# The transposes behind a batch of 32x32 inverses, 22 products later on TensorE; their copies and scalings ahead of a key norm's second half

## Chip, cores and metric

The kernel runs on one core of a Trainium2 chip. The metric is device microseconds of one launch, by the median of several runs. One execution is profiled as well; its time is longer than the span of its trace by what lies around the span.

## The reference

One layer of a diffusion transformer over 1024 latent tokens and 256 context tokens, width 1024, in fp32. After a modulated RMS norm there is one input projection. Half of its columns feed a gated DeltaNet (4 heads of 128, chunked, forward and backward), the other half a neighbourhood attention (8 heads of 64). Output projection, a gated residual and a SwiGLU feed-forward network follow. What matters here:

```python
# gated DeltaNet, by chunk: the inverse of a unit triangular matrix
m = jnp.where(strict, jnp.einsum("bhncd,bhnmd->bhncm", kb, k) * decay, 0.0)
a_mat = jnp.eye(CHUNK, dtype=f32) + m
u = lax.linalg.triangular_solve(a_mat, v * beta[..., None], left_side=True, lower=True, unit_diagonal=True)
w = lax.linalg.triangular_solve(a_mat, kb * jnp.exp(gam)[..., None], left_side=True, lower=True, unit_diagonal=True)
# neighbourhood attention: q and k are normalised by head
q = rms_norm(q, q_norm_w) * NA_HEAD_DIM ** -0.5
k = rms_norm(k, k_norm_w)
```

## The kernel before

**Products.** An fp32 product is made of three products of rounded parts: hh x whi, hl x whi, hh x wlo. The input projection goes by jobs; a `Block` is 128 columns of weights against all tokens, with eight K steps. A block without context tokens makes two matmuls of 128x512 in each of the three products of a step, 48 in all; each of them is called a product below. A block fills `blk` banks of PSUM (4 in all).

**Order of the jobs.** k0 to k3, a wide job, nk0, nk1, nk2, the other wide job (the attention's values), nk3, nq0, nq1, nq2, q0, then q1 to q3, v0 to v3, nq3, z0 to z3. The nk and nq blocks are keys and queries of the attention, and are normalised. Around the change stand nk3, nq0, nq1, nq2, q0 and q1.

**A block's steps.** `mm` makes the products. `evac` copies the banks to `cacc` on ACT (L491; L506 for q). `silu` squares into `cr` (L532). `norm`, called after the next block's products, sums the squares on PE (a matmul with a constant for each piece of 256 or 512 columns), takes Ln (L549) and Exp (L551, L553) on ACT, then multiplies on DVE (L556), splits the result in two f16 halves (ACT L561 or L568, DVE L562 or L569), and sends four stores (L574) to nk_d or nq_d. Each Ln reads its piece from a PSUM bank that `bank()` gives: an "m" bank, of which there are two from nk0 on, or a "pr" bank, also two, for a key's last piece.

**Weights.** For each block SP loads `wraw` (L218, one buffer), ACT casts it to `whi` (L219), and POOL makes `wlo` (L221); `whi` and `wlo` have two buffers each.

**Behind the values.** After the second wide job, 16 copies from DRAM to DRAM (`windows`, L1095) are put out on SP's queue, two after each K step.

**Background work.** Two generators run piece by piece beside the blocks, one piece (`yield`) after each K step up to q0, three after that. `block_inverses` builds the 32x32 diagonal blocks, inverts all of them at once by a chain of 60 steps on DVE (L947, L949) in the tile N, then turns the result back with 32 transposes on PE (L106, four in each "m" bank), eight copies on DVE (L961, into WK), two stream transposes (L967) and two scalings by beta (L970) on DVE, and four stores to x_d (L969, L972). `preps` comes next: for each direction and chunk it fetches e, kk and xc (L997 to L999; xc comes from x_d), fills fx on ACT (L1011) and y on POOL (L1012), makes decays on ACT (L1015), multiplies kk by them on DVE (L1016), and runs four fx matmuls into "pr" with a copy on ACT (L1028), and three rounds of four y matmuls with copies on DVE (L1036). Two or three chunks are alive at a time.

**What sets the order.** A scheduler orders each engine's instructions by priority, which by default is program order, and then each engine runs its own list in that order. `high_priority(offset=n)` moves instructions up, `keep_in_program_order` pins an instruction to its place among the others of its engine, and `issue_after` holds instructions back until another has been placed.

Of the kernel before, what the change touches and what calls it, by code (L numbers as in the profile page):

```python
# [9 lines left out]
F32 = mybir.dt.float32  # L10
# [4 lines left out]
OP = mybir.AluOpType  # L15
# [12 lines left out]
NU = NCH * NH  # L28
# [63 lines left out]
def hybrid(ctx, tc, a, dbg):  # L92
    nc = tc.nc
    act, dve, pool, sp = nc.scalar, nc.vector, nc.gpsimd, nc.sync
# [14 lines left out]
    pe = Tensor()  # L109
# [33 lines left out]
    ident = M[C_ID]  # L143
# [27 lines left out]
    x_d = dram.tile([128, 2, 2, NU, 32], F32, name="x_d", tag="x_d")  # L171
# [17 lines left out]
    NB = const("NB", [128, 2, NCH, 4])  # L189
# [5 lines left out]
    bg = Background()  # L195
# [69 lines left out]
    fl = lambda x: x.rearrange("p a b -> p (a b)")  # L265
# [155 lines left out]
    with ExitStack() as bs:  # L421
# [32 lines left out]
        class Block:  # L454
# [79 lines left out]
            def norm(self):  # L534

                kind, acc, t0, i = self.kind, self.acc, self.t0, self.i
                if kind in "vz":
                    return
                if kind == "k":
                    sp.dma_start(kT_d[:, i], acc)  # L540
                    return
                r = self.r
                if kind == "q":
                    sp.dma_start(qT_d[:, i], acc[:, t0:])
                    return
                for s0, n in self.segs:
                    p = bank("pr" if kind == "nk" and s0 >= 768 else "m")
                    pe.matmul(p[:, :n], M[C_BD2], r[:, s0:s0 + n], start=True, stop=True)
                    act.activation(r[:, s0:s0 + n], p[:, :n], AF.Ln, bias=b_eps, scale=1.0 / ND)  # L549
                if kind == "nq":  # L550
                    act.activation(r[:, t0:], r[:, t0:], AF.Exp, scale=-0.5, bias=b_naq)  # L551
                else:
                    act.activation(r[:, t0:], r[:, t0:], AF.Exp, scale=-0.5)  # L553
                isk = kind == "nk"
                u = acc
                dve.scalar_tensor_tensor(u[:, t0:], u[:, t0:], qkw[:, isk:isk + 1], r[:, t0:],  # L556
                                         op0=OP.mult, op1=OP.mult)
                hl16 = cp.tile([128, 2, T], F16, name="hl16", tag="kx", bufs=3)
                h16, l16 = hl16[:, 0], hl16[:, 1]
                if isk:  # L560
                    act.copy(h16, u)  # L561
                    dve.tensor_tensor(l16, u, h16, OP.subtract)  # L562
                else:
                    for hf in range(2):
                        s = slice(t0 + hf * 512, t0 + hf * 512 + 512)
                        uv = u[:, s].rearrange("p (r b c) -> p b r c", r=8, b=4)
                        hv, lv = (x[:, s].rearrange("p (b r c) -> p b r c", b=4, r=8) for x in (h16, l16))
                        act.copy(hv, uv)  # L568
                        dve.tensor_tensor(lv, uv, hv, OP.subtract)  # L569
                for i, x in enumerate((h16, l16)):  # L570
                    for hb in range(2):
                        hd = 2 * self.i + hb
                        dst = nk_d[i, hd] if isk else nq_d[hd, i]
                        sp.dma_start(dst, x[hb * 64:hb * 64 + 64, t0:])  # L574
# [99 lines left out]
        first = [Block("k", 0), Block("k", 1)]  # L674
        with ExitStack() as xs:
# [12 lines left out]
            for k in range(KT):  # L688
                x = xp.tile([128, T], F32, name=f"xt{k}", tag=f"xt{k}")
# [95 lines left out]
            split = "split"  # L785
# [101 lines left out]
        def block_inverses():  # L887
            with ExitStack() as gs:
# [3 lines left out]
                N = gp.tile([128, 4, 32, 32], F32, name="N", tag="N")  # L892
                P = 2 * NU
                fl = lambda x: x.rearrange("p u i -> p (u i)")
                with ExitStack() as g3s:
# [18 lines left out]
                    for i, (d, u0, n) in enumerate(cuts):  # L914
                        rcs, nxt = nxt, rhs(*cuts[i + 1]) if i + 1 < len(cuts) else None
                        p = bank()
# [33 lines left out]
                    yield  # L950
                flat = N.rearrange("p b r c -> p b (r c)")
                dve.memset(flat[:P, :, 0:1024:33], 1.0)
                for _ in range(1):
                    yield
                U = WK.rearrange("p d u i -> p (d u) i")
                for i0 in range(0, 32, 4):
                    p = bank()
                    for i in range(4):
                        pe.transpose(p[:, i * P:(i + 1) * P], N[:P, :, :, i0 + i].rearrange("p b r -> p (b r)"),
                                     ident[:P, :P])  # L960
                    dve.tensor_copy(U[:, :, i0:i0 + 4], p[:, :4 * P].rearrange("p (i u) -> p u i", i=4))  # L961
                    if i0 % 8 == 4:
                        yield
                for d in range(2):
                    ud = U[:, d * NU:(d + 1) * NU]
                    ut = g4.tile([128, NU, 32], F32, name="ut", tag="ut")
                    dve.transpose(fl(ut), fl(ud))  # L967
                    x, s = (ut, ud) if d else (ud, ut)
                    sp.dma_start(x_d[:, d, 0], x)  # L969
                    dve.tensor_tensor(s, s, NB[:, d].rearrange("p c (h o) -> p (c h) o", o=1).to_broadcast(  # L970
                        [128, NU, 32]), OP.mult)
                    sp.dma_start(x_d[:, d, 1], s)  # L972
                    yield

        done = set()

        def preps():

            first_half.close()
            with ExitStack() as gs:  # L980
# [11 lines left out]
                def fetch(d, c):  # L992

                    kk, xc = work("kk", 5), pp.tile([128, 2, 4, 32], F32, name="xc", tag="xc", bufs=3)
                    e = work("e", 4)
                    u = (d * NCH + c) * 4
                    sp.dma_start(fl(e), g_d[u:u + 4].rearrange("h t -> (h t)").partition_broadcast(128))  # L997
                    sp.dma_start(kk, kk_d[:, c])
                    sp.dma_start(xc, x_d[:, d, :, c * 4:c * 4 + 4])  # L999
                    at = None  # L1000
                    if c >= 2:
                        at = work("at", 4)
                        sp.dma_start(at, qk_d[:, c - 2])
                    return d, c, kk, xc, e, at
# [49 lines left out]
                todo = [(d, ORDER[d][i]) for i in range(NCH) for d in range(2)]  # L1054
                live, landing = [], []
                n = 0
                while live or todo or landing:
                    while len(landing) < 2 and todo and (todo[0][1] < 2 or all(x in done for x in queries)):
                        landing.append([fetch(*todo.pop(0)), False])
                    if landing and len(live) < 3:  # L1060
                        triangle(landing[0])
                        live.append(prep(n, *landing.pop(0)[0]))
                        n += 1
                        if landing:
                            triangle(landing[0])
                    if not live:
                        yield
                    nxt = []
                    for g in live:
                        tick[0] += 1  # L1070
                        flush(tick[0])
                        if next(g, 0):
                            nxt.append(g)
                        yield
                    live = nxt
# [9 lines left out]
        values = inv + 3  # L1085
        queries = range(turn - 1, later)
        jobs += [Block("v", i) for i in range(4)] + [Block("nq", 3)]
        gates = len(jobs)
        jobs += [Block("z", i) for i in range(4)]

# [15 lines left out]
        first[0].evac()  # L1106
        first[0].silu()
        first[1].evac()
        first[0].norm()
        first[1].silu()  # L1110
        for n in range(2, len(jobs) + 2):
            j = jobs[n] if n < len(jobs) else None
# [27 lines left out]
            if isinstance(j, Wide):  # L1140
                for t, _ in enumerate(j.tiles()):
                    next(fin, 0)
                    for _ in range(3):
                        next(taps, 0)
                    if t == 4 and nrm:
                        nrm.norm()
                        for _ in fin:
                            pass
                        fin = nrm.finish()
                        done.add(n - 1)  # L1150
                        nrm = None
                    bg2.step(2)
                    if n < turn:
                        bg.step(2)
                    if n >= turn:
                        bg.step(5)
            elif j:
                for k in range(KT):
                    j.mm([k])
                    next(taps, 0)  # L1160
                    next(taps, 0)
                    if k >= 3:
                        next(fin, 0)
                    bg.step(1 if n < turn else 3)
                    bg2.step(1)
                    copies.step(2)
                j.evac()
            for _ in fin:
                pass
# [1 line left out]
            if isinstance(j, Wide) and n == values:  # L1171
                copies.add(windows())
            if nrm:
                nrm.norm()
            if isinstance(j, Block) and j.later is None:
                j.silu()

# [395 lines left out]
    with ExitStack() as us:  # L1573
# [13 lines left out]
        def split(x, src, k):  # L1587
            act.copy(x[0][:, k], src[:, k])
            dve.tensor_tensor(x[1][:, k], src[:, k], x[0][:, k].bitcast(F32), OP.subtract)  # L1589
# [274 lines left out]
```

## Time and profile before

| what | us |
|---|---|
| runs before | 1516.0, 1511.06, 1514.58 |
| their median | 1514.58 |
| the profiled execution | 1507.78 |
| its span | 1506.0 |
| mean granted TensorE clock of the profiled execution | 0.994 of full speed |

A row of the timeline has the start and duration in us, the engine, the line and operation, output<-inputs with the tile's size and the number of instructions that it groups, and in brackets how long the engine had been idle and which instruction ended that. The span of a group covers its instructions from first to last, and matmuls overlap, so the distance of two starts says more than a duration. PE is TensorE's matrix product, DVE the vector engine, ACT the scalar engine, POOL GpSimd; SP (SPq for its queue) issues the DMAs. Lines of the profile before are those of the kernel before; in the changed kernel the same instructions stand 5 to 14 lines further down (L556 is L561, L561 is L566, L568 is L573, L961 is L968, L967 and L970 are L976 and L979, L1011 is L1021, L1016 is L1026, L1028 is L1038).

### The profile page before, as it was taken

The numbers are of one execution on the slowest core, as the hardware profiler recorded it, in microseconds if no ns is written. First come the engines' busy times: TensorE is split into PE (matmuls) and PEld (weight loads), VectorE is DVE, ScalarE is ACT, GpSimd is POOL, SyncE is SP. The second block draws the span as 40 slices with busy tenths as digits, with TensorE's granted clock in tenths as the row PEclk, the third lists the DMA queues.
The fourth block names the chain that finished last, engine by engine and source line by source line (L and its number), as shares of the span: only waits on it lengthen the run. The fifth ranks groups of instructions, "written<-read, shape, count | busy, mean of one in ns | idle before, by whom it ended". The sixth has DMA issues, their size and how long they took to land.

```text
span 1506.0 us, 23093 instructions
## 1 busy us (share of the span) xinstructions
PE 1449.8 (96%) x8365; PEld 1201.0 (80%) x8365; DVE 1004.4 (67%) x1892; ACT 696.2 (46%) x1321; POOL 193.4 (13%) x223
## 2 busy tenths in 40 slices
PE   5999998899999999999989999999999999999998
PEld 2789787678877778887877878888888888888887
DVE  4886579455598427679966499666655557698642
ACT  6443461584266526566742374333333334354440
POOL 0154500343124221211100000000000000000000
PEclk9999999999999999999999999999999999999999
DMA  9377133555377799986349106333333334898742
GB/s 368 117 234 239 57 92 121 191 168 190 118 243 238 220 284 265 262 228 193 110 134 332 72 30 203 113 105 105 102 102 105 106 105 161 287 349 286 240 145 84
DMA packets 198851, 267.35 MB, mean 178 GB/s; under 512 B 15232, under 2 KB 106960, under 8 KB 197712
## 3 DMA queue, kind: packets, MB, share of 16 engines
q1 hardware_dynamic: 198016, 265.49, 54.7%
q8 instruction: 66, 1.08, 0.3%
q14 instruction: 49, 0.40, 0.1%
q10 hardware_dynamic: 720, 0.37, 0.1%
HBM read 201.01 MB, written 68.98 MB: 179 GB/s over the span
## 4 chain that ended last, share of the span: by engine, by line
PE 51%; DVE 6%; ACT 3%; DMA 2%; issue 1%; SPq 0%; ACTq 0%; DVEq 0%
PE ps L102 45%; PE sc L102 5%; PE sc L106 2%; DMA wad<-wa 1%; ACT pt L377 1%; ACT ex L365 1%; DVE ex L363 1%; DVE acc L255 1%; DVE x L1618 1%; DVE x L1594 0%; DVE ex L367 0%; DVE ulo L1449 0%; DVE lT L1589 0%; DVE ws L1444 0%; ACT x L1598 0%
## 5 line engine op out<-in xcount | busy, mean ns | idle before, releaser
L102 PE MATMUL ps<-hT,uhi 128*128 128x512 f32 x496 | 146.8, 390 | 0.8 <-DVE e L1739 0.7
L102 PE MATMUL ps<-lT,uhi 128*128 128x512 f32 x496 | 146.4, 389 | 0.0
L102 PE MATMUL ps<-hT,ulo 128*128 128x512 f32 x496 | 146.3, 389 | 0.0
L102 PE MATMUL blk<-hh,whi 128*128 128x512 f32 (+1 forms) x456 | 138.0, 393 | 2.4 <-ACT hh L748 1.7
L102 PE MATMUL blk<-hh,wlo 128*128 128x512 f32 (+1 forms) x456 | 129.7, 377 | 0.0
L102 PE MATMUL ps<-hB,uhi 128*128 128x512 f32 x436 | 129.1, 390 | 0.0
L102 PE MATMUL blk<-hl,whi 128*128 128x512 f32 (+1 forms) x456 | 129.0, 376 | 0.0
L102 PE MATMUL ps<-lB,uhi 128*128 128x512 f32 x436 | 128.8, 389 | 0.0
L102 PE MATMUL ps<-hB,ulo 128*128 128x512 f32 x436 | 128.8, 389 | 0.0
L1448 ACT CAST uhi<-ws 128x512 fp32r<-128x512 f32 x91 | 54.7, 622 | 145.5 <-PE ps L102 78.2
L1448 ACT CAST uhi<-wq 128x512 fp32r<-128x512 f32 x101 | 60.4, 621 | 132.8 <-PE ps L102 69.4
L1449 DVE TENSOR_TENSOR ulo<-wq,uhi 128x512 fp32r<-128x512 f32 x101 | 67.1, 687 | 65.6 <-ACT uhi L1448 36.4
L102 PEld LDWEIGHTS ps<-hT,uhi 128*128 128x128 f32 x496 | 93.0, 188 | 20.7 <-ACT uhi L1448 1.1
L102 PEld LDWEIGHTS ps<-lT,uhi 128*128 128x128 f32 x496 | 93.0, 188 | 19.7 <-DVE lT L1602 0.5
L102 PEld LDWEIGHTS ps<-hT,ulo 128*128 128x128 f32 x496 | 93.1, 188 | 19.4
L102 PEld LDWEIGHTS ps<-hB,uhi 128*128 128x128 f32 x436 | 81.8, 188 | 17.5 <-issue 0.5
L102 PEld LDWEIGHTS ps<-lB,uhi 128*128 128x128 f32 x436 | 81.8, 188 | 17.3 <-DVE lB L1602 0.4
L102 PEld LDWEIGHTS ps<-hB,ulo 128*128 128x128 f32 x436 | 81.8, 188 | 17.0
L102 PEld LDWEIGHTS blk<-hh,wlo 128*128 128x128 f32 x456 | 80.1, 189 | 17.6 <-issue 1.7
L102 PEld LDWEIGHTS blk<-hl,whi 128*128 128x128 f32 x456 | 80.7, 189 | 15.5
L102 PEld LDWEIGHTS blk<-hh,whi 128*128 128x128 f32 x456 | 76.5, 189 | 19.8 <-ACT hh L748 3.7
L1449 DVE TENSOR_TENSOR ulo<-ws,uhi 128x512 fp32r<-128x512 f32 x91 | 60.6, 685 | 36.2 <-ACT uhi L1448 28.0
(341 smaller groups left out, 3026.0 us busy)
## 6 DMA issues: line engine op xcount, KB each, us to landing
wq<-w_fo SPq DMA_DIRECT2D x99, 256.0 KB
wq<-w_gu SPq DMA_DIRECT2D x88, 256.0 KB
wad<-wa SPq DMA_DIRECT2D x64, 256.0 KB
t_d<-g SPq DMA_DIRECT2D x22, 512.0 KB
fr<-t_d SPq DMA_DIRECT2D x44, 256.0 KB
bt<-rpb SPq DMA_DIRECT2D x48, 192.0 KB
f_d<-g SPq DMA_DIRECT2D x33, 256.0 KB
fr<-f_d SPq DMA_DIRECT2D x33, 256.0 KB
```

Source lines behind the costliest of these rows:

```text
L102: i = nc.tensor.matmul(*args, **kw)
L106: i = nc.tensor.transpose(*args, **kw)
L255: dve.scalar_tensor_tensor(acc2, x, sc, acc2, op0=OP.mult, op1=OP.add)
L363: dve.tensor_tensor_reduce(ex, sc, bt, 1.0, -3.0e38, OP.add, OP.max, m[:, 0:1])
L365: act.activation(ex, ex, AF.Exp, bias=m[:, 1:2], accum_out=m[:, 2:3])
L377: act.copy(pt, sc)
L1448: act.copy(hi, self.raw[key])
L1449: dve.tensor_tensor(lo, self.raw[key], hi.bitcast(F32), OP.subtract)
L1618: dve.tensor_tensor(B[at][:, k], B[x][:, k], B.get(y, B["B11"])[:, k], OP.subtract)
```

## The change

The transposes leave eight pieces after the inverses' last step instead of one, and are pinned to program order; their copies, the stream transposes and the scalings get a higher priority. The stream transposes write into N's memory instead of a new tile. `norm` is cut in two: the part up to the Exp, and `split`, which multiplies, casts and stores. While the inverses aren't done, nk3's `split` is kept back until the first chunk's fetch has been put into the program, and then follows the last scaling; for the other blocks up to q0 `split` follows the last scaling too. The first two chunks' fetches come ahead of the rest of `preps` by three pieces, and from q1 on a block's last K step runs four pieces of background work.

```diff
-                isk = kind == "nk"
+                return self.split
+
+            def split(self):
+
+                acc, t0, i, r = self.acc, self.t0, self.i, self.r
+                isk = self.kind == "nk"
                 u = acc
                 dve.scalar_tensor_tensor(u[:, t0:], u[:, t0:], qkw[:, isk:isk + 1], r[:, t0:],
                                          op0=OP.mult, op1=OP.mult)
...
-                for _ in range(1):
+                for _ in range(8):
                     yield
                 U = WK.rearrange("p d u i -> p (d u) i")
                 for i0 in range(0, 32, 4):
                     p = bank()
                     for i in range(4):
-                        pe.transpose(p[:, i * P:(i + 1) * P], N[:P, :, :, i0 + i].rearrange("p b r -> p (b r)"),
-                                     ident[:P, :P])
-                    dve.tensor_copy(U[:, :, i0:i0 + 4], p[:, :4 * P].rearrange("p (i u) -> p u i", i=4))
+                        tc.keep_in_program_order(nc.tensor.transpose(
+                            p[:, i * P:(i + 1) * P], N[:P, :, :, i0 + i].rearrange("p b r -> p (b r)"),
+                            ident[:P, :P]))
+                    with tc.high_priority(offset=400):
+                        dve.tensor_copy(U[:, :, i0:i0 + 4], p[:, :4 * P].rearrange("p (i u) -> p u i", i=4))
                     if i0 % 8 == 4:
                         yield
-                for d in range(2):
-                    ud = U[:, d * NU:(d + 1) * NU]
-                    ut = g4.tile([128, NU, 32], F32, name="ut", tag="ut")
-                    dve.transpose(fl(ut), fl(ud))
...
-                    yield
+                with tc.high_priority(offset=400):
+                    for d in range(2):
+                        ud = U[:, d * NU:(d + 1) * NU]
+                        ut = N.rearrange("p b r c -> p (b r c)")[:, d * 1280:(d + 1) * 1280].rearrange(
+                            "p (u i) -> p u i", i=32)
+                        dve.transpose(fl(ut), fl(ud))
+                        x, s = (ut, ud) if d else (ud, ut)
+                        sp.dma_start(x_d[:, d, 0], x)
+                        end = dve.tensor_tensor(s, s, NB[:, d].rearrange("p c (h o) -> p (c h) o", o=1).to_broadcast(
+                            [128, NU, 32]), OP.mult)
+                        sp.dma_start(x_d[:, d, 1], s)
+                inverse[:] = [end]
+                yield
...
-                    sp.dma_start(xc, x_d[:, d, :, c * 4:c * 4 + 4])
+                    started.append(sp.dma_start(xc, x_d[:, d, :, c * 4:c * 4 + 4]))
...
+                landing += [[fetch(*todo.pop(0)), False] for _ in range(2)]
+                for _ in range(3):
+                    yield
                 while live or todo or landing:
...
-                    bg.step(1 if n < turn else 3)
+                    bg.step(1 if n < turn else 4 if k == 7 else 3)
                     bg2.step(1)
                     copies.step(2)
+                if waiting:
+                    while not started:
+                        bg.step(1)
+                    with tc.issue_after(inverse[0].ins):
+                        waiting.pop()()
                 j.evac()
...
             if nrm:
-                nrm.norm()
+                rest = nrm.norm()
+                if nrm is tail and not inverse:
+                    waiting.append(rest)
+                else:
+                    with tc.issue_after(inverse[0].ins) if inverse and n < turn else ExitStack():
+                        rest()
```

Here `tail` is nk3. The other two calls, `first[0].norm()` and the one in the wide job, become `norm()()`.

The first place is on PE, at the end of nq0's products and the start of nq1's. Before (hh_136 begins a block, so the last rows are nk3's norm and the first products of nq1):

```order
L102 MATMUL blk<-hh_419,whi 128x512 x2
L106 MATMUL m<-cst,N 128x80 x2
L102 MATMUL blk<-hl_420,whi 128x512 x2
L102 MATMUL blk<-hh_419,wlo 128x512
L106 MATMUL m<-cst,N 128x80 x6
L102 MATMUL blk<-hh_419,wlo 128x512
...
L102 MATMUL blk<-hh_423,wlo 128x512 x2
L102 MATMUL m<-cr,cst 128x256
L102 MATMUL m<-cr,cst 128x512
L102 MATMUL pr<-cr,cst 128x512
L102 MATMUL blk<-hh_136,whi 128x512 x2
```

In the changed kernel, from the end of nq0:

```order
L102 MATMUL blk<-hh_423,wlo 128x512 x2
L102 MATMUL m<-cr,cst 128x256
L102 MATMUL m<-cr,cst 128x512
L102 MATMUL pr<-cr,cst 128x512
L102 MATMUL blk<-hh_136,whi 128x512 x2
L102 MATMUL blk<-hl_137,whi 128x512 x2
L102 MATMUL blk<-hh_136,wlo 128x512 x2
L964 MATMUL m<-cst,N 128x80 x8
L102 MATMUL blk<-hh_138,whi 128x512 x2
L102 MATMUL blk<-hl_139,whi 128x512 x2
L102 MATMUL blk<-hh_138,wlo 128x512 x2
L964 MATMUL m<-cst,N 128x80 x8
```

The transposes have moved from ahead of nk3's norm to behind it, with 16 products of nq0 and six of nq1 in front; two more groups of eight follow after six products each.

The second place is on ACT, from the cast of nq2's weights to the first chunk's decays. In the changed kernel:

```order
L219 CAST whi<-wraw 128x1024
L491 ACTIVATE cacc<-blk 128x512 x2
L549 ACT_TABLE_LOAD
L549 ACTIVATE cr<-m,bias 128x256
L549 ACTIVATE cr<-m,bias 128x512
...
L219 CAST whi<-wraw 128x1024
L549 ACT_TABLE_LOAD
L549 ACTIVATE cr<-m,bias 128x512 x2
L551 ACT_TABLE_LOAD
L551 ACTIVATE cr<-cr,bias 128x1024
L566 CAST hl_2568<-cacc 128x1280
L573 CAST hl_2586<-cacc 128x512 x2
```

and what follows it there, with the evacuation and the square of nq1 between the chunk's pieces:

```order
L491 ACTIVATE cacc<-blk 128x512 x2
L1021 COPY fx_2535<-xc 32x4x32
L532 ACTIVATE cr<-cacc 128x1024
L1021 COPY fx_2535<-xc 32x4x32 x3
L1025 ACTIVATE e<-e,GN 128x128 x4
```

Up to L549 of nk3 the order is that of before. Behind it, before has L561, L219, L491, L549, L551 and then the chunk's copies; now nk3's cast follows nq0's Exp, and nq1's evacuation stands ahead of the chunk.

More of the change, by code (lines that the diff above doesn't have):

```diff
@@ L537, in norm @@
                 if kind in "vz":
-                    return
+                    return int
                 if kind == "k":
                     sp.dma_start(kT_d[:, i], acc)
-                    return
+                    return int
                 r = self.r
@@ L544, in norm @@
                     sp.dma_start(qT_d[:, i], acc[:, t0:])
-                    return
+                    return int
                 for s0, n in self.segs:
@@ L958, in block_inverses @@
                     for i in range(4):
-                        pe.transpose(p[:, i * P:(i + 1) * P], N[:P, :, :, i0 + i].rearrange("p b r -> p (b r)"),
-                                     ident[:P, :P])
-                    dve.tensor_copy(U[:, :, i0:i0 + 4], p[:, :4 * P].rearrange("p (i u) -> p u i", i=4))
+                        tc.keep_in_program_order(nc.tensor.transpose(
[3 more added lines that the diff above has]
+                        dve.tensor_copy(U[:, :, i0:i0 + 4], p[:, :4 * P].rearrange("p (i u) -> p u i", i=4))
                     if i0 % 8 == 4:
                         yield
-                for d in range(2):
-                    ud = U[:, d * NU:(d + 1) * NU]
-                    ut = g4.tile([128, NU, 32], F32, name="ut", tag="ut")
-                    dve.transpose(fl(ut), fl(ud))
[L968 to L972, printed above, removed]
-                    yield
-        done = set()
+                with tc.high_priority(offset=400):
[11 more added lines that the diff above has]
+                yield
+        done, inverse, waiting, started = set(), [], [], []
         def preps():
@@ L1087, in hybrid @@
         jobs += [Block("v", i) for i in range(4)] + [Block("nq", 3)]
+        tail = jobs[values + 1]
         gates = len(jobs)
@@ L1108, in hybrid @@
         first[1].evac()
-        first[0].norm()
+        first[0].norm()()
         first[1].silu()
@@ L1145, in hybrid @@
                     if t == 4 and nrm:
-                        nrm.norm()
+                        nrm.norm()()
                         for _ in fin:
@@ L1173, in hybrid @@
             if nrm:
-                nrm.norm()
+                rest = nrm.norm()
[4 more added lines that the diff above has]
+                        rest()
             if isinstance(j, Block) and j.later is None:
```

## The prediction

> **What bounds the kernel now.** I read the page's first part, then the list of what TensorE (PE) waits for, then the timelines of PE, ACT, DVE and SP around the two waits that the change aims at, and last the granted clock there.
>
> ```profile
> span 1506.0 us, 23093 instructions
> PE 1449.8 (96%) x8365; PEld 1201.0 (80%) x8365; DVE 1004.4 (67%) x1892; ACT 696.2 (46%) x1321; POOL 193.4 (13%) x223
> ```
>
> PE is busy for 96% of the span, so time comes off only where PE idles or runs at half clock. In the list of waits (in all, times, longest) two belong to the inverses and the chunk preparation:
>
> ```profile
> PE pr L102 <- DVE kk L1016: 6.9, 1, 6.9
> PE m L106 <- DVE N L952: 5.4, 1, 5.4
> ```
>
> The first of them in time stands inside the block nq0 (start, duration, what runs, and in brackets the idle time before):
>
> ```profile
> 256.38 0.61 PE L102 MATMUL blk<-hh,whi 128*128 128x512 f32 x2
> 262.41 0.53 PE L106 MATMUL m<-cst,N 80*128 80x80 f32 x2 [5.42 <-DVE N L952]
> 262.67 1.20 PE L102 MATMUL blk<-hl,whi 128*128 128x512 f32 x2
> 263.67 0.63 PE L102 MATMUL blk<-hh,wlo 128*128 128x512 f32 x1
> ...
> 267.06 0.48 PE L102 MATMUL blk<-hl,whi 128*128 128x512 f32 x1
> ...
> 267.74 0.49 PE L102 MATMUL blk<-hl,whi 128*128 128x512 f32 x1
> ...
> 271.27 1.45 PE L102 MATMUL m<-cr,cst 128*128 128x256 f32 x4
> ...
> 273.02 1.04 PE L102 MATMUL blk<-hh,whi 128*128 128x512 f32 x2
> 273.90 0.63 PE L102 MATMUL blk<-hl,whi 128*128 128x512 f32 x2
> 274.37 0.62 PE L102 MATMUL blk<-hh,wlo 128*128 128x512 f32 x2
> ```
>
> Five sizes come out of these starts. A warm pair of products takes about 0.455 (0.47 from 273.90 to 274.37), a product 0.2275. A cold pair takes 1.00 (262.67 to 263.67). Four transposes and a product take 0.68 (267.06 to 267.74), so eight transposes about 0.9. The norm of nk3 takes 1.75 (271.27 to 273.02). From 262.41 to 271.27 there are 32 transposes and 16 products: 8.86, of which the products are worth 16 x 0.2275 = 3.64, so transposes and cold clock cost 5.22.
>
> The second wait stands at the first chunk's matmuls, in nq2:
>
> ```profile
> 284.37 1.88 PE L102 MATMUL m<-cr,cst 128*128 128x512 f32 x4
> 299.09 2.02 PE L102 MATMUL pr<-fx,kk 128*128 128x96 f32 x8 [6.90 <-DVE kk L1016]
> ...
> 309.41 1.03 PE L102 MATMUL pr<-fx,kk 128*128 128x96 f32 x8
> 310.37 0.85 PE L102 MATMUL pr<-y,kk 128*32 128x96 f32 x8
> ...
> 315.15 1.03 PE L102 MATMUL blk<-hh,whi 128*128 128x512 f32 x2
> ```
>
> So the stretch that the change can touch runs from 256.38 to 315.15, where q0 starts. The granted clock in it, by single microseconds (the number behind the busy times is the clock):
>
> ```profile
> 259.00:260.00 1.00, 0.00 (x0) 0.00 (x0) 0.94 (x2) 0.00 (x0) 0.00 (x0) 0.82 0.26 100
> 266.00:267.00 1.00, 1.00 (x10) 0.98 (x9) 0.40 (x1) 0.00 (x0) 0.00 (x0) 0.76 0.80 264
> 297.00:298.00 1.00, 0.00 (x0) 0.00 (x0) 0.00 (x0) 1.00 (x5) 0.49 (x1) 0.60 1.02 338
> ```
>
> A share of 0.82 means full speed until 259.64, which is 2.6 us after PE stopped at 262.41 - 5.42 = 256.99; in the second wait the drop came at 297.2, 5.0 us after the stop at 292.19. After the restart at 262.41 full speed came back at about 266.5, 4.1 us later.
>
> **First part: the transposes.** Behind hh,whi at 256.38, which ends its slot at 256.83, PE now goes straight on: 16 products (3.64) to 260.47, nk3's norm (1.75) to 262.2, six products of nq1 (1.37) to 263.6. The wait of 5.42 is gone by then, since N's chain ended on DVE about 263. But what is late next is the place that the transposes write to. They take an "m" bank; there are two, and by the new order nk3's norm has just filled both. They come free when ACT's L549 has read them. ACT:
>
> ```profile
> 273.49 1.05 ACT L219 CAST whi<-wraw 128x1024 fp32r<-128x1024 f32 x1 [20.93 <-DMA wraw<-w_nqk]
> 274.45 1.08 ACT L491 ACTIVATE cacc<-blk 128x512 f32<-128x512 f32 x2
> 275.54 1.28 ACT L549 ACT_TABLE_LOAD   x1
> 276.83 1.05 ACT L549 ACTIVATE cr<-m,bias 128x256 f32<-128x256 f32 x2
> ```
>
> L549 stands in ACT's order, before and after, behind the cast of nq2's weights, and that one waited 20.93 us for their load. What holds the load is on SP's queue:
>
> ```profile
> 249.66 11.61 SPq L1095 DMA_DIRECT2D vw_d<-nv_d  x5
> 261.36 2.26 SPq L218 DMA_DIRECT2D wraw<-w_nqk  x1
> ```
>
> The window copies vw_d go out ahead of it in both versions; the change moves neither. In before nobody noticed: the transposes ran ahead of nk3's norm, when the banks were empty. Now they stand behind it, so PE waits from 263.6 to about 277.2 (the first of the two L549 is the short one, about 0.4): **13.6 us in place of 5.42**. Queued behind them on PE is the rest of nq1, 42 products, and all after it.
>
> From 277.2: eight transposes, the second bank coming free at 277.9, to about 278.4; six products at half clock (3.0) to 281.4, where the clock is back (277.2 + 4.1); then 24 transposes (2.0 to 2.7) and 36 products (8.19) to 291.6 to 292.3. I take 292.0. Before, that point (nq1's end) was 284.37. So the first part costs **+7.6**. Its bounds: the load of nq2 landing 0.6 earlier, as the x_d stores no longer run beside its end, +7.0; transposes paced by the eight copies on DVE, +8.3. The copies (L968 now, ahead on DVE by priority) lie beside these 36 products.
>
> **Second part: the scalings, nk3's second half, the first chunks.** Before, from 284.37 to 315.15 there are 30.8 us. The work in it is about 20.3: nq0's and nq1's norms (1.75 x 1024/1280 = 1.4 each), 48 products of nq2 (10.92), and some 6.6 of chunk matmuls (for sizes see 309.41: four fx matmuls 0.96; 310.37 and below: a round of y up to 0.8). So 10.5 is overhead: 6.90 of waiting, 2 of half clock behind it, 1.6 in small pieces. What is it after? PE reaches the first fx matmuls after 1.4 of norm and 42 products (9.56) instead of 26, at 303.0. They need the copies fx and DVE's L1026, and those stand at the end of this ACT chain (durations from before):
>
> ```profile
> 283.62 1.26 ACT L561 CAST hl<-cacc 128x1280 f16<-128x1280 f32 x1 [1.62 <-DVE cacc L556]
> 288.90 1.27 ACT L549 ACTIVATE cr<-m,bias 128x512 f32<-128x512 f32 x2
> 290.06 1.06 ACT L532 ACTIVATE cr<-cacc 128x1024 f32<-128x1024 f32 x1
> 292.43 1.15 ACT L551 ACTIVATE cr<-cr,bias 128x1024 f32<-128x1024 f32 x1
> 295.35 1.25 ACT L1011 COPY fx<-xc 32x128 f32<-32x128 f32 x4 [1.77 <-DMA xc<-x_d]
> 296.63 1.57 ACT L1015 ACTIVATE e<-e,GN 128x128 f32<-128x128 f32 x5
> 301.84 1.14 ACT L568 CAST hl<-cacc 128x512 f16<-128x512 f32 x2
> ```
>
> and of DVE, whose two scalings and stream transposes (L976, L979, 1.5 each) end about 293 to 295, ahead of nk3's L561:
>
> ```profile
> 272.18 1.49 DVE L970 TENSOR_TENSOR ut<-ut,NB 128x1280 f32<-128x1280 f32 x1
> 286.32 3.70 DVE L970 TENSOR_TENSOR WK<-WK,NB 128x1280 f32<-128x1280 f32 x1
> 298.34 0.69 DVE L1016 TENSOR_TENSOR kk<-kk,e 128x512 f32<-128x512 f32 x1 [3.45 <-DMA nk_d<-hl]
> ```
>
> The cast of q0's weights waits for nq1's last product with whi, about 291.7. From there: cast 1.05, table 1.28, L549 1.27, table 1.28, L551 1.15 (297.7); nk3's cast 1.26 (299.0); nq0's casts 1.14; L491 waits for nk3's residual on DVE, which follows nq0's scaling (299.0 + 1.5), then 1.08 (301.6); L1021 and L532 2.31; four e of the row's 1.57 for five, 1.26 (305.2); L1026 0.69: **305.9**. The wait is 2.9. One L970 took 3.70 where the other took 1.49; if that repeats, it is hidden by the chain above, which DVE meets only at 297.7. Were that cover gone it would cost 2.2.
>
> Two more waits appear, as ACT's order now has the evacuation and the norm of the next block ahead of the next chunks' pieces. For the third chunk's fx: from nq2's last product ACT does L491 1.08, a copy 0.5, L532 1.06, two tables 2.56, L549 1.27, L551 1.15, four e and four fx 2.5, casts 1.14, then DVE 0.69: 11.95, against PE's 10.3 (fx 0.96, norm 1.4, 31 products 7.05, two rounds of y about 0.9). That is 1.7, 2.2 with what is left over from the first. For the fourth chunk the same kind of chain, with a weight cast and three e more, is 12.4 against 10.2: 2.2. In all 2.9 + 2.2 + 2.2 and small pieces 0.9: 8.2 in place of 10.5, **-2.3**.
>
> Moved as well: nk3's four and nq0's four stores to nk_d and nq_d now follow the first two chunks' fetches on SP's queue, and ahead of the third's.
>
> ```profile
> 290.94 0.85 SPq L999 DMA_DIRECT2D xc<-x_d  x1
> 294.97 1.11 SPq L574 DMA_DIRECT2D nk_d<-hl  x2
> ```
>
> Eight issues at 0.55 are 4.4 us, from 300 on; a fetch was used 4.4 us after its issue (290.94 to 295.35). The third chunk's data land about 309.5, and are used about 313: hidden. The attention that reads nk_d and nq_d comes much later. The first chunk's own fetch goes out behind the scalings, about 296, and lands by 300.5, ahead of L1021 at 301.6. The memory of ut now lies in N, which nobody reads by then. Behind q1 the orders are the same but for a few chunk pieces.
>
> **Clock.** A wait of 2.9 stands close to the 2.6 after which the clock fell once and under the 5.0 of the other time; 2.2 stands under both. I take nothing for it; if the first of them halves the clock it adds 2 (before's second wait), if all do, up to 4. [...]
>
> **Sum.** +7.6 - 2.3 = +5.3, with bounds of -2.9 (the second part's overhead all gone: 7.6 - 10.5) and about +12 (clock, DVE's 2.2, the upper bound of the first part). The profiled run took 1507.78 with the span of 1506.0 in it, so it would become 1513.1. It lies 6.8 under the median of the runs, 1514.58; with the same difference the median becomes **1519.9, say 1520**.
>
> **Rivals.**
> 1. The transposes wait as told, but the second part becomes smooth: chunks find their fx ready. For it: PE arrives 3.9 us later than before at the first fx (303.0 against 299.09) and the wait was 6.90 from 292.19. Against it: ACT's chain is 14.2 long from nq1's end. 7.6 - 10.5 = -2.9: 1511.7, no measurable change.
> 2. The change does what it says: both waits go, the banks are free in time. This takes L549 to have read by 263.6, 13.6 us earlier than the rows; it decides for "faster" only if nq2's weights land by about 260, with the vw_d copies still in front. -5.42 - 2 (cold) - 6.9 = -14: 1500.
> 3. As the forecast, with the small waits halving the clock and DVE's 2.2 in the open: +9 to +12, 1524 to 1527.
>
> **How the numbers follow.** Differences under about 0.3%, 4.5 us, can't be told from no change. Forecast 0.64, of it 0.45 over +4.5 and 0.19 within; rival 1 0.15, within; rival 2 0.09, faster; rival 3 0.12, slower. That makes faster 0.09, same 0.34, slower 0.57. The range goes from just below rival 1 (1510) to the upper end of rival 3 (1527), which leaves out rival 2 and some of the tails.
>
> **What would show it.** Right: a wait of 13 to 14 us of PE at the first L964 transposes, put down to ACT's L549, with half clock behind it; no wait on N; a wait of about 3 us on DVE L1026, and two of 2 us later. Wrong: L549 well before 277, transposes without a wait; or a wait of over 5 us still at the first fx. If the first wait is there and the total is no slower, the second part was mis-sized.

## The result and the profile after

| | runs | median, us | lowest to highest |
|---|---|---|---|
| before | 7 | 1511.06 | 1508.67 to 1516.0 |
| changed | 7 | 1519.26 | 1518.09 to 1525.14 |

The ratio is 1.0057, with a 95% interval of 1.0036 to 1.0078: the change makes the kernel 8.2 us slower. Forecast were +5.3 us and 1520. The profiled execution of the changed kernel took 1521.18 us, with a span of 1519.4.

What TensorE waits for in the changed kernel between 240 and 362 us (in all, times, longest):

```profile
PE m L964 <- ACT cr L549: 13.3, 1, 13.3
PE pr L102 <- DVE kk L1026: 3.5, 2, 2.5
PE pr L102 <- ACT kk L1038: 3.3, 1, 3.3
```

The waits of 5.4 and 6.9 are gone; in their place stand four. Their places in PE's timeline:

```profile
264.69 0.62 PE L102 MATMUL blk<-hh,wlo 128*128 128x512 f32 x2
278.58 1.37 PE L964 MATMUL m<-cst,N 80*128 80x80 f32 x8 [13.27 <-ACT cr L549]
279.69 1.20 PE L102 MATMUL blk<-hh,whi 128*128 128x512 f32 x2
280.68 1.05 PE L102 MATMUL blk<-hl,whi 128*128 128x512 f32 x2
...
294.14 1.88 PE L102 MATMUL m<-cr,cst 128*128 128x512 f32 x4
...
308.06 1.53 PE L102 MATMUL pr<-fx,kk 128*128 128x96 f32 x8 [2.48 <-DVE kk L1026]
...
324.75 1.10 PE L102 MATMUL pr<-fx,kk 128*128 128x96 f32 x8 [1.04 <-DVE kk L1026]
...
345.62 0.44 PE L102 MATMUL pr<-y,kk 128*32 128x32 f32 x8 [3.25 <-ACT kk L1038]
...
360.38 1.84 PE L102 MATMUL m<-ones,cr 128*128 128x1 f32 x16
```

And on ACT the cast that everything stands behind, with the load that it waits for:

```profile
250.11 1.05 ACT L219 CAST whi<-wraw 128x1024 fp32r<-128x1024 f32 x1 [13.14 <-PE blk L102]
...
274.71 1.04 ACT L219 CAST whi<-wraw 128x1024 fp32r<-128x1024 f32 x1 [20.99 <-DMA wraw<-w_nqk]
275.66 1.08 ACT L491 ACTIVATE cacc<-blk 128x512 f32<-128x512 f32 x2
276.76 1.28 ACT L549 ACT_TABLE_LOAD   x1
278.05 1.05 ACT L549 ACTIVATE cr<-m,bias 128x256 f32<-128x256 f32 x2
```

The first transposes start some 0.5 us after L549 does, and L549 starts 3.3 us after the cast. To compare traces I measure from the cast of nq1's weights (here 250.11), which stands ahead of the change, to the start of nq0's norm (294.14, where nq1 ends), and from there to the first matmul with ones in v0's part (360.38), behind which both run alike for a while. In the kernel before the two outer marks are:

```profile
248.94 1.05 ACT L219 CAST whi<-wraw 128x1024 fp32r<-128x1024 f32 x1 [13.14 <-PE blk L102]
```

```profile
349.55 1.84 PE L102 MATMUL m<-ones,cr 128*128 128x1 f32 x16
```

With 284.37 between them, before has 35.4 and 65.2 us, 100.6 in all; the changed kernel 44.0 and 66.2, 110.3 in all. So the first part costs 8.6 us and the second 1.1, together 9.7. Beyond the two outer marks the profiled runs differ by another 3.7 us: 1.2 ahead, where both kernels run the same order, and 2.6 behind. For 83.6 us behind the second mark TensorE runs the same order in the same time; then some of the chunks' matmuls come in other places, so that a part of the 2.6 may still be the change's. The medians differ by 8.2.

### The profile page after: what moved, and what is told of

Its sections match the earlier page's. It is cut to its first block, busy times and chain, and to the rows that moved or that the text cites. A ratio compares the mean times of both kernels' runs of the same rounds, so it can differ in the third digit from the quotient of the medians.

```text
span 1519.4 us, 23101 instructions
## 1 busy us (share of the span) xinstructions
PE 1453.8 (96%) x8365; PEld 1204.4 (79%) x8365; DVE 1008.0 (66%) x1892; ACT 699.5 (46%) x1323; POOL 197.4 (13%) x223
## 4 chain that ended last, share of the span: by engine, by line
PE 51%; DVE 5%; ACT 3%; DMA 2%; issue 1%; SPq 0%; ACTq 0%; DVEq 0%
PE ps L102 44%; PE sc L102 5%; PE sc L106 2%; DMA wad<-wa 1%; ACT pt L377 1%; ACT ex L365 1%; DVE acc L255 1%; DVE ex L363 1%; DVE x L1642 1%; DVE x L1618 0%; DVE ulo L1473 0%; DVE lT L1613 0%; DMA zT_d<-zt 0%; DMA wraw<-w_out 0%; ACT x L1622 0%
```

## The experiments

Two theories. **Banks**: the time goes at the transposes, which wait for the two m banks that nk3's norm holds, since L549 is queued on ACT behind a cast whose weights come late. **Second half**: the time goes where the key norm's second half and the chunks were rearranged. All results in one table; the marks are those just defined, from each kernel's profiled run, and each ratio is against the kernel before on the same chip.

| kernel | cast to nq1's end | from there to the ones | both | median, us | ratio to before (95%) |
|---|---|---|---|---|---|
| before | 35.4 | 65.2 | 100.6 | | |
| changed | 44.0 | 66.2 | 110.3 | 1519.26 | 1.0057 (1.0036 to 1.0078) |
| e1: Ln ahead of the cast | 28.8 | 71.3 | 100.1 | 1510.67 | 1.0004 (0.9989 to 1.0020) |
| e2: load ahead of the copies | 33.7 | 66.6 | 100.3 | 1510.63 | 1.0000 (0.9987 to 1.0012) |
| e3: transposes at their old place | 35.6 | 68.1 | 103.7 | 1514.71 | 1.0027 (1.0016 to 1.0038) |
| e4: before, transposes moved | 43.8 | 61.4 | 105.2 | 1513.88 | 1.0028 (1.0017 to 1.0039) |
| g1: changed, both remedies | 28.8 | 66.8 | 95.6 | 1504.71 | 0.9955 (0.9939 to 0.9971) |
| g2: e4, both remedies | 31.9 | 62.0 | 93.9 | 1502.87 | 0.9950 (0.9933 to 0.9967) |
| g3: before, both remedies | 35.5 | 68.6 | 104.1 | 1513.03 | 1.0017 (1.0000 to 1.0034) |
| g4: changed, second half at once | 44.1 | 63.1 | 107.2 | 1519.33 | 1.0061 (1.0037 to 1.0085) |
| h1: g4, both remedies | 30.6 | 65.4 | 96.0 | 1505.20 | 0.9959 (0.9942 to 0.9976) |
| h2: g2, copies by priority | 31.8 | 64.6 | 96.4 | 1504.17 | 0.9977 (0.9964 to 0.9989) |
| h3: short hold, both remedies | 28.8 | 66.6 | 95.4 | 1503.09 | 0.9957 (0.9943 to 0.9972) |
| k1: e3 without early fetches | 35.4 | 68.3 | 103.7 | 1510.49 | 1.0007 (0.9992 to 1.0021) |

The medians of before in the four series were 1510.46 (e), 1511.51 (g), 1510.29 (h) and 1510.36 (k).

**e1: nk3's Ln ahead of the cast.**

```diff
-            act.copy(h, r)
+            with tc.issue_after(hold[0].ins) if hold else ExitStack():
+                act.copy(h, r)
...
+                hold[:] = [jobs[n - 2].ln] if n == values + 3 else []
                 jobs[n + 1].prefetch()
+                hold[:] = []
```

`ln` is the norm's last L549. Expected:

> The changed kernel, with ACT's cast of nq2's weights held behind the three Ln of nk3's norm; nothing else. Theory (banks): the change costs time because the transposes wait for the two m banks that nk3's norm holds, and these are read late only because L549 stands behind that cast. Then TensorE's wait at the first transposes shrinks from 13.3 us to 0 to 1.5 us, with full clock behind it, and nq1 ends about 15 us earlier than in the changed kernel. q0's weights are loaded no earlier than before, so the chunk preparation starts late and the wait at the first fx matmuls grows from 2.5 us to about 7. In sum 9 to 10 us less than the changed kernel: about 1510. Rival (second half): the loss comes from the key norm's second half and the chunks behind it, and a wait taken away at the transposes only moves there: the wait goes but the time stays within 3 us of the changed kernel, 1517 to 1522.

PE's timeline of e1 (line numbers three higher):

```profile
265.96 0.68 PE L967 MATMUL m<-cst,N 80*128 80x80 f32 x4 [0.30 <-ACT cr L552]
...
278.83 1.88 PE L102 MATMUL m<-cr,cst 128*128 128x512 f32 x4
...
296.82 2.02 PE L102 MATMUL pr<-fx,kk 128*128 128x96 f32 x8 [6.55 <-DVE kk L1029]
```

and its ACT:

```profile
263.90 0.47 ACT L552 ACTIVATE cr<-m,bias 128x256 f32<-128x256 f32 x1
...
274.60 1.05 ACT L222 CAST whi<-wraw 128x1024 fp32r<-128x1024 f32 x1 [8.12 <-DMA wraw<-w_nqk]
...
282.62 1.05 ACT L222 CAST whi<-wraw 128x1024 fp32r<-128x1024 f32 x1 [4.38 <-DMA wraw<-w_conv]
```

The cast still comes at 274.6, but TensorE doesn't wait for it: the 13.3 shrink to 0.3, and nq1 ends 15.2 us earlier. A third of that is lost again, as expected: q0's weights go into the buffer that nq2's have just left, so their cast now waits 4.38 for its own load, and with it the first fx, 6.55. The rival, that the wait only moves, falls: the time is 8.6 us below the changed kernel's.

**e2: the load ahead of the window copies.**

```diff
                 for ch in range(4):
-                    sp.dma_start(vw_d[:, cb, ch], vlat[4 * ch:4 * ch + 4, BLKS[cb]:BLKS[cb] + 32])
+                    while cb * 4 + ch >= 11 and not ahead:
+                        yield
+                    with tc.issue_after(ahead[0].ins) if cb * 4 + ch >= 11 else ExitStack():
+                        sp.dma_start(vw_d[:, cb, ch], vlat[4 * ch:4 * ch + 4, BLKS[cb]:BLKS[cb] + 32])
                     yield
...
+                if n == values + 3:
+                    ahead[:] = loaded
```

`ahead` holds the load of nq2's weights, once it has been put out. Expected:

> The changed kernel, with the last five of the 16 window copies issued behind the load of nq2's weights instead of ahead of it; the orders on TensorE and ACT stay. Theory (banks): the load lands 8 to 11 us earlier, the cast and L549 follow it, and the wait at the first transposes shrinks by as much, from 13.3 to 2 to 5.5 us, with some half clock left. Total 8 to 11 us below the changed kernel, about 1510. Rival 1: the load is slow by itself and not because of the copies ahead of it; then it lands as late as before and the wait stays at 13. Rival 2 (second half): the wait shrinks and the total stays within 3 us of the changed kernel.

SP, ACT and PE of e2 in that order:

```profile
256.19 0.61 SPq L220 DMA_DIRECT2D wraw<-w_nqk  x1
256.85 10.08 SPq L1114 DMA_DIRECT2D vw_d<-nv_d  x5
```

```profile
264.46 1.05 ACT L221 CAST whi<-wraw 128x1024 fp32r<-128x1024 f32 x1 [10.62 <-DMA wraw<-w_nqk]
```

```profile
268.33 1.38 PE L966 MATMUL m<-cst,N 80*128 80x80 f32 x8 [2.88 <-ACT cr L551]
```

The cast moves from 274.71 to 264.46, 10.3 us earlier, and the wait shrinks by 10.4, from 13.27 to 2.88, with ACT's and PE's orders untouched. So the load's landing sets this wait, and the copies ahead of it set the landing.

**e3: only the transposes back at their old place.** The edit is `range(8)` to `range(1)` in the changed kernel.

> The changed kernel with the transposes one piece behind the inverses' last step again, so ahead of nk3's norm; priorities, the split norm and the early fetches stay. Theory (banks): no wait on L549; instead the wait of about 5.4 us on N as before the change, and nq1 ends where it did before. The chunk's copies and decays now stand ahead of nq1's evacuation on ACT, and the wait at the first fx should be about 2 us in place of 6.9. Total 3 to 6 us below the kernel before: about 1506. Rival (second half): the split and the moved fetches are what costs; then this kernel stays slower than the kernel before, 1515 or more.

This expectation missed by 9 us. The wait on N is back with 5.43, as told, but the first fx still wait 6.3:

```profile
289.98 1.88 PE L102 MATMUL m<-cr,cst 128*128 128x512 f32 x4
...
298.67 2.02 PE L102 MATMUL pr<-fx,kk 128*128 128x96 f32 x8 [6.34 <-DVE kk L1026]
```

The first chunk is ready 8.7 us behind nq1's end, against 14.7 in the kernel before (299.09 less 284.37); but TensorE now comes to it after two products of nq2 instead of 26. An earlier chunk that was also ordered earlier gains nothing, and a wait of 2.4 at the fourth chunk came on top. The rival, 1515 or more, stands closer to the 1514.71 than my figure. But only 3.0 us of it lie between the marks in the profiled run; that run also lost time well ahead of them, at a mean granted clock of 0.82 against 1.00, in code that the kernels share. The 15 us from 150 on, of e3 and of the kernel before (granted clock third from the right):

```profile
150.00:165.00 15.00, 13.19 (x61) 10.98 (x60) 10.31 (x44) 1.29 (x7) 8.14 (x13) 0.82 0.16 45
```

```profile
150.00:165.00 15.00, 14.17 (x78) 11.79 (x77) 8.06 (x40) 2.92 (x9) 8.25 (x15) 1.00 0.17 48
```

How many of e3's other runs have that, the profile of one doesn't say.

**e4: only the transposes moved.** The kernel before with `range(8)` and the pinned transposes.

> The kernel before with only the transposes moved: eight pieces instead of one, pinned to program order. Theory (banks): TensorE waits 13 us for nk3's L549 at the first transposes, just as in the changed kernel, and nq1 ends 8 to 9 us later than before. The first fx now stand behind all of nq2 and nq1's norm, so that the wait there (6.9 us before) may vanish: between 1511 and 1519, say 1515. Rival (second half): with the second half where it was, moving the transposes costs nothing: no wait over 3 us at the transposes, and a time at or below the kernel before.

```profile
277.81 1.38 PE L959 MATMUL m<-cst,N 80*128 80x80 f32 x8 [12.97 <-ACT cr L549]
...
293.44 1.88 PE L102 MATMUL m<-cr,cst 128*128 128x512 f32 x4
...
309.73 1.13 PE L102 MATMUL pr<-fx,kk 128*128 128x96 f32 x8 [1.76 <-DVE kk L1017]
```

The wait is there in full, 12.97, and so is the first part's cost (43.8 against 35.4). The fx wait falls to 1.76, since they stand behind 48 products, and the second part gives 3.8 us back. So by the medians the moved transposes alone (1.0028) cost about as much as the rest of the change alone (e3, 1.0027), and the whole change as much as both (1.0057).

**g1 to g3: both remedies, with the whole change, with the delay alone, and without any of it.**

> The changed kernel with both remedies of the first runs: ACT's cast of nq2's weights behind nk3's Ln, and the last five window copies behind the load of these weights. Theory (banks): no wait at the transposes as with the first remedy alone, and q0's weights now come in time, so that the wait at the first fx goes back from 6.5 to about 3 us. From the cast of nq1's weights to the first matmul with ones (100.6 us in the kernel before, 110.3 in the changed one) 95 us: about 1505, 5 us below the kernel before. Rival: the wait at the first fx stays at 6 or more because ACT's chain from nq1's end is the limit whatever the loads do; then 100 us and no gain over the first remedy, 1510.

> The kernel before with the transposes moved by eight pieces and pinned, and both remedies; the key norm's second half, priorities and fetches as before the change. Two theories on the second part. If the change's own second part (split norm, priorities, early fetches) costs about 5 us, as the stretch behind nq1's end says (61.4 us with the delay alone, 66.2 in the changed kernel), this kernel saves the first part's cost and that too: a stretch of 90 to 92 us, 1500 to 1502. If the short second part of the delay alone is only time won back because everything there was already late, it grows to 66 or more here and the kernel is no better than the one with both remedies on the changed kernel, 1505.

> The kernel before with both remedies and nothing of the change. If the remedies work by freeing the banks for moved transposes, they gain little here: the wait of 5.4 us on N stays, and only the wait at the first fx shrinks as ACT's chain runs earlier, from 6.9 to 3 to 5 us; 1506 to 1509. If they gain as much here as with moved transposes, the place of the transposes doesn't matter: 1500 to 1503.

g1 came out as expected: q0's cast now waits for nq1's products and not for its load, and the first fx wait 3.02 us. g2 lies close to the first of its two answers: the short second part stays (62.0), but the stretch of 93.9 and the median of 1502.87 are above the 90 to 92 and 1500 to 1502 told. Both rows are g1's:

```profile
278.22 1.05 ACT L224 CAST whi<-wraw 128x1024 fp32r<-128x1024 f32 x1 [9.07 <-PE blk L102]
```

```profile
292.45 1.13 PE L102 MATMUL pr<-fx,kk 128*128 128x96 f32 x8 [3.02 <-DVE kk L1031]
```

With the place of the transposes as in the change and the banks free, the kernel is 7 to 9 us faster than before; of the two, g2, without the rest of the change, has the lower ratio, but the intervals overlap widely. g3 was expected at 1506 to 1509 and isn't faster than before at all. The fx wait shrinks to 4.51 as told, but a later one appears, and the wait on N stays:

```profile
297.45 2.02 PE L102 MATMUL pr<-fx,kk 128*128 128x96 f32 x8 [4.51 <-DVE kk L1021]
...
337.24 1.49 PE L102 MATMUL pr<-y,kk 128*32 128x96 f32 x8 [3.04 <-DVE y L1041]
```

So the remedies gain nothing by themselves; they pay because the transposes moved.

**g4, h1: the second half at once.** In the changed kernel, without and with the remedies:

```diff
-                if nrm is tail and not inverse:
-                    waiting.append(rest)
-                else:
-                    with tc.issue_after(inverse[0].ins) if inverse and n < turn else ExitStack():
-                        rest()
+                rest()
```

> The changed kernel with nk3's second half (and nq0's) put out at once again, without the hold and without the wait for the scaling; transposes, priorities and early fetches stay changed. Wait of 13 us at the transposes in any case. If the held-back second half is what makes the second part slow, it shortens from 66.2 to 61 to 63 us, and the time goes from 1519 to about 1514 to 1515. If the early fetches and priorities do it, the time stays at 1518 to 1520.

> The changed kernel with both remedies, and the second halves of nk3's and nq0's norms put out at once, without hold. Two effects against each other, by the traces so far: held back, nk3's L561 does not stand between the transposes' copies on DVE (nq1 ends 28.8 us behind the cast of its weights, 31.9 where it stands there); but the second part is longer by 3 to 5 us. If both are real this kernel lies between the two earlier ones: nq1's end at 31 to 32, second part 62 to 63.5, 1503 to 1505. If the hold costs nothing in the second part, that stays at 66 to 67 and the time is 1507 or 1508.

By the marks the hold costs 3.1 us in the second part without the remedies (66.2 against 63.1). But g4's median, of six runs, is the changed kernel's; the question stays open there. With the remedies the two effects cancel: held back, nk3's L561 stays out of the copies' way on DVE (28.8 against 30.6), and costs 1.4 behind (66.8 against 65.4); g1 and h1 have the same time. h1's second part was told as 62 to 63.5, so here the hold costs less than half of what its trace without the remedies said. The hold is not what makes the change slow.

**h2, h3: looking for the good of both.** h2 gives g2's copies the change's priority. h3 holds nk3's second half only until the last copy, puts nq0's out at once, and has no early fetches; of its edit against g1, the first:

```diff
+                if waiting:
+                    with tc.issue_after(copied[0].ins):
+                        waiting.pop()()
```

> The kernel before with the transposes moved, both remedies, and of the change's other parts only the priority of the transposes' copies. DVE's order still has nk3's scaling behind the first two copies, so TensorE should still wait 1 to 1.5 us for a copy: nq1's end at 31 to 32, second part 62 as without the priority, 1502 to 1503. If the priority alone cures that wait: nq1's end at 29, 1500.

> Moved transposes and both remedies, nk3's second half held back only until the last of the eight copies (not until the scalings and the first fetch), nq0's second half at once, no early fetches. If the hold helps by keeping DVE free for the copies and harms by putting nk3's cast and nq1's evacuation ahead of the first chunk on ACT, this has the good of both: nq1's end at 28.8, second part 62 to 63, a stretch of 91 to 92 against 100.6 before, 1500 to 1502. If the harm comes with any hold: second part 66, 1505.

Priority alone doesn't bring nk3's L561 out from between the copies (31.8), as expected; its second part is 2.6 longer than g2's in the profile, where 62 was told. h3 has the short first part, and the second was missed (66.6 against 62 to 63): the first fx wait only 0.65, but at the fourth chunk there is

```profile
327.40 0.64 PE L102 MATMUL pr<-y,kk 128*32 128x32 f32 x8 [5.57 <-ACT kk L1042]
```

ACT's order has the next chunk's decays and another block's casts ahead of that chunk's copy, and for these decays ACT stood 3.06 us until POOL had masked e:

```profile
324.47 0.40 ACT L1029 ACTIVATE e<-e,GN 128x128 f32<-128x128 f32 x1 [3.06 <-POOL e L1058]
```

Neither beats g2.

**k1: e3 without the early fetches.**

```diff
-                landing += [[fetch(*todo.pop(0)), False] for _ in range(2)]
-                for _ in range(3):
-                    yield
...
-                    bg.step(1 if n < turn else 4 if k == 7 else 3)
+                    bg.step(1 if n < turn else 3)
```

> The changed kernel with the transposes one piece behind the inverses' last step, and without the early fetches, their three pieces and the fourth piece of a last K step: of the change only priorities, the memory of ut and the hold are left. Asked is what in the rest of the change costs some 4 us when the transposes stay. If it is the early fetches, which let the chunks' pieces spread behind the next block's evacuation on ACT, the wait of 2.4 at the fourth chunk goes and the second part returns from 68 to 65 or 66 us: 1510 to 1512. If it is the priority, which draws the scalings and with them the first fx ahead on TensorE, the second part stays at 67 to 69: 1514. The wait of 6.3 at the first fx should stay in both cases, since these stand behind two products of nq2 in either.

The time came out as the first answer had it, and the stretch as the second: 1510.49, but 68.3 us in the second part, with 7.86 at the first fx. So between the marks k1 and e3 are alike (103.7 both), and the 4 us by which their medians differ lie elsewhere or in runs that weren't profiled. What the rest of the change costs when the transposes stay, 0 to 4 us, and which part of it, is left open.

## Why the prediction held, and where its sizes were off

- *The wait that takes the place of the one removed.* Foretold 13.6 on nk3's L549, measured 13.27. e1 and e2 show both halves of the cause: take the cast out of L549's way, or let the load land earlier, and the wait goes to 0.3 or 2.9. e4 shows that moving the transposes is enough to make it.
- *First part, +7.6.* Measured +8.6. The mis-sized term is the half clock behind the wait: taken as 4.1 us after the restart, it lasted from the restart at 278.58 until 284.74 (worked out below), 6.2 us. Half of the 2.1 more is the missing 1.0. The 4.1 was read from one restart and is no fixed length, as the last section shows.
- *Second part, -2.3.* Measured +1.1. The three small waits were foretold as 2.9, 2.2 and 2.2, 7.3 in all, and came as 2.48, 1.04 and 3.25, 6.8 in all. What failed is the step "I take nothing for it": the clock was halved behind the first and the last of them, for 3.42 and 3.40 us. At half speed that costs an estimated 1.7 each, 3.4 in all, as much as the difference of -2.3 and +1.1; the 0.5 by which the waits came out shorter must have gone elsewhere, which no run here separates. The bound of up to 4 for the clock was on record; the choice between the ends was wrong. The comparison behind that choice was wrong too: 2.6 and 5.0 us are the times from TensorE's stop to the fall of the clock, inside waits of 5.42 and 6.90, and don't say how long a wait has to be.
- *The rivals.* That the change does what it says would have needed the banks free in time; e1 shows what that is worth, 15 us in the first part. A second part without waits was seen in no run. The third, with the clock, is what came in the second part, but without DVE's 2.2: L976 and L979 ran at 1.45 to 1.5 each.
- *Sum.* +9.7 in the stretch of the profiled run against +5.3; +8.2 in the medians. By these estimates the clock is the larger part of both misses. That the median of the changed kernel met the forecast of 1520 so closely is luck: the forecast started from a median of before (three runs, 1514.58) that seven runs then put at 1511.06; the difference was forecast 3 us too low.

## What to carry to other kernels

Before an instruction is moved, ask what it takes besides its data: here its input was ready 14 us before (DVE ended N at 264.40, the transposes started at 278.58), but its PSUM banks were with an earlier user, whose reader was queued on another engine behind a cast whose weights came late. The reader's place in that queue was a dependency too (ahead of the cast, in e1, the wait is 0.30 in place of 13.27); follow it to its end (PE, then ACT, then the load, then the copies ahead on the DMA queue, where e2 takes off 10.4), since the cheapest repair may lie there: two changes of order, on ACT and SP, turned a loss of 8 us into a gain of 7. And a stall that was taken away early paid only as far as the next producer could keep up: of the 15.2 us that e1 won, 5.1 were lost again at the first fx and behind, until the second remedy brought q0's weights in time.

## What the runs showed of the hardware

The granted clock, and the waits around its falls. In the changed kernel these single microseconds hold all changes of the granted clock (third number from the right) in the stretch; the second row stands for those between the first fall and the first rise:

```profile
267.00:268.00 1.00, 0.00 (x0) 0.00 (x0) 0.00 (x0) 0.00 (x0) 0.00 (x0) 0.83 0.98 316
268.00:269.00 1.00, 0.00 (x0) 0.00 (x0) 0.00 (x0) 0.00 (x0) 0.00 (x0) 0.50 0.28 109
...
284.00:285.00 1.00, 1.00 (x4) 0.81 (x3) 0.19 (x1) 0.00 (x0) 0.00 (x0) 0.63 0.00 0
...
308.00:309.00 1.00, 0.94 (x7) 0.94 (x7) 0.01 (x1) 0.98 (x5) 0.00 (x0) 0.81 0.67 150
...
312.00:313.00 1.00, 1.00 (x7) 0.92 (x8) 0.25 (x1) 0.54 (x2) 0.77 (x3) 0.98 1.02 344
...
346.00:347.00 1.00, 1.00 (x5) 0.81 (x4) 0.97 (x3) 0.97 (x4) 0.00 (x0) 0.59 0.60 127
...
349.00:350.00 1.00, 1.00 (x5) 0.79 (x3) 0.24 (x1) 0.99 (x2) 0.00 (x0) 0.71 0.67 256
```

From each fall to the next rise it is 0.50, elsewhere in the stretch 1.00. A share of 0.83 in a microsecond in which it goes from 1.00 to 0.50 then means full speed for 0.66 of it. So the clock fell at 267.66, 308.62 and 346.18, and rose at 284.74, 312.04 and 349.58. The first fall lies inside the wait of 13.27 us, 2.35 after TensorE's stop at 265.31. The other two came behind waits of 2.48 and 3.25, each 0.56 us after TensorE had gone on. e4 has a fall behind a wait of 1.76 (307.97 to 309.73; the clock falls at 311.34, 1.6 us after it):

```profile
311.00:312.00 1.00, 1.00 (x5) 0.67 (x3) 0.00 (x0) 0.98 (x3) 0.89 (x2) 0.67 1.03 364
312.00:313.00 1.00, 1.00 (x10) 0.50 (x8) 0.00 (x0) 0.95 (x4) 0.85 (x4) 0.50 0.80 254
```

while g2 kept full clock behind a wait of 2.40:

```profile
327.86 0.44 PE L102 MATMUL pr<-y,kk 128*32 128x32 f32 x8 [2.40 <-ACT kk L1034]
```

```profile
328.00:329.00 1.00, 1.00 (x11) 0.86 (x10) 1.00 (x3) 0.95 (x4) 1.00 (x1) 1.00 0.99 384
...
330.00:331.00 1.00, 1.00 (x6) 0.70 (x4) 0.94 (x3) 0.04 (x1) 0.93 (x1) 1.00 0.68 166
```

and had products at half speed behind one of only 1.47:

```profile
270.54 1.11 PE L964 MATMUL m<-cst,N 80*128 80x80 f32 x8 [1.47 <-DVE WK L967]
...
273.42 1.20 PE L102 MATMUL blk<-hh,whi 128*128 128x512 f32 x2
274.42 1.05 PE L102 MATMUL blk<-hl,whi 128*128 128x512 f32 x2
...
276.31 0.63 PE L102 MATMUL blk<-hh,whi 128*128 128x512 f32 x2
276.78 0.62 PE L102 MATMUL blk<-hl,whi 128*128 128x512 f32 x2
```

```profile
272.00:290.00 18.00, 18.00 (x75) 13.98 (x74) 9.99 (x9) 8.37 (x10) 5.19 (x7) 0.91 0.64 222
```

The granted clock is 0.91 in the mean of these 18 us. The pair at 273.42 takes 1.00, as the one at 279.69 in the changed kernel takes 0.99 at a granted clock of 0.50; the pair at 276.31 takes 0.47. So in these traces the length of a wait doesn't tell by itself whether the clock falls behind it: 1.47, 1.76, 2.48 and 3.25 had half speed behind them, 2.40 had not. Nor was the time from TensorE's restart to full clock the same each time: 4.1 us behind the first wait of the kernel before, 6.2 behind the long one of the changed kernel, and 3.98 and 3.96 behind its other two (308.06 to 312.04, 345.62 to 349.58). What decides either is not shown; no run changes such a wait alone.
